# Seven products instead of eight for pairs of groups in the first and last feed-forward half-layers

## The chip, the cores and the metric

One Trainium2 chip, one of its cores. The metric is the time of one execution in microseconds (us) of device time. Times of before: three runs, median 942.07 us.

## The reference, cut to what matters

Two decoder layers over 256 tokens of 1024 features in fp32. Each layer is a half feed-forward, a mixer, and another half feed-forward; that makes four feed-forward halves, numbered f = 0 to 3 in the kernel. The change touches halves 0 and 3.

```python
def _rmsnorm(x, g):
    y = x * lax.rsqrt(jnp.mean(x * x, axis=-1, keepdims=True) + EPS)
    return y * g
def _swiglu(h, w_gate, w_up, w_down):
    return (jax.nn.silu(h @ w_gate) * (h @ w_up)) @ w_down
...
    x = x + 0.5 * _swiglu(_rmsnorm(x, ffn_norm[layer, 0]), ffn_w_gate[layer, 0],
                          ffn_w_up[layer, 0], ffn_w_down[layer, 0])
```

The hidden width is 2816. The first mixer is attention with pooling, the second an S5 state-space layer with a GLU behind it.

## The kernel before

**Tiling.** The 256 tokens are two tiles of 128 (t = 0, 1). The normalized activations stand in `hn[t]` by rows and, transposed, in `hTh` and `hTl`. Every fp32 factor is cut into a high part of reduced precision (fp32r) and the rest, and a product is three products of parts: high by high, high by rest, rest by high. For a weight, ScalarE copies the loaded tile `raw` into `wh` (the high part, line 182) and VectorE subtracts it from `raw` into `wl` (line 139). The factor `rstd` of the norm is applied after the product.

**Groups.** A feed-forward half goes over 11 groups g of 256 hidden columns. For each group and token tile, `gate_up` multiplies the activations by the gate and up columns together (512 columns), in two halves `kh` of the contraction, 4 x 3 matmuls of 128x512 in each half, into a PSUM tile `wk`. Then ScalarE makes `sg` = silu(gate x rstd) (line 436), VectorE makes `pr` = up x rstd x sg (line 148), `hid_T` transposes `pr` on TensorE into `sk` and splits it into `hh` and `hl`, and `down` multiplies these by 256 rows of the down matrix into `acc`, 24 matmuls for the group. `ffn_joint` puts the down products of the group before behind the gate and up products of this one.

**Weights.** A weight unit is 1 MB: gate and up columns of one group and one half of the contraction (`f`), or 256 rows of the down matrix (`d`). It is loaded by two DMAs of 512 KB from SP's queue into `raw` (four buffers) and split by two copies and two subtractions of 128x1024 into `wh` and `wl` (`RING` = four buffers of each). `pump`, called ahead of every step, issues the loads and splits of the next units in the order of first use, as far as the four-deep ring allows: a unit can be split when the unit four before it has had its last use.

**Order.** The program is traced as a list of steps. The order of each engine's queue is then fixed when the program is built: a scheduler goes through its own model of time, and an idle engine gets, among the instructions whose data and buffers are ready, the one with the best priority, which is the one traced first; `prio(n)` moves an instruction n places forward, `behind(...)` pins it behind others on its engine. On the chip each queue runs in that order. VectorE's and ScalarE's work on products (`sg`, `pr`, `hh`, `hl`) carries `prio(CHAIN)` and goes ahead of the splits. PSUM has two `wk` and two `sk` buffers.

**Around the change.** Half 0 begins with `first`, which loads x and the first weights; group 0 follows in separate steps, then `ffn_joint(0, 1, 4)`, a step `opened` that opens the mixer's memory, issues its ten small loads and computes the rotary tables, and `ffn_joint(0, 4, NG)`. Half 3 follows the GLU of the S5 layer: its memory is released, `head(3, "f3")` does group 0, and `ffn_joint(3, 1, NG)` the rest. The weights of the GLU (`in_s_w_glu`) are loaded through the same `raw` buffers.

Of the kernel before, what the change touches and what calls it, by code (L numbers as in the profile page):

```python
# [17 lines left out]
DM = 1024  # L18
# [20 lines left out]
    p600 p101 s10 p610 p701 e00 p601 s11 x10 p710 T00 p611 t10 x11 g0 p711 s00 t12 g1 p400 x00 p401 m0 t01 p410  # L39
    p510 m1 t00 p500 v00 t11 p411 p511 G1 p501 v10 G0 t13 v01 v11 V0 V1 o20 o21 o31 o30  # L40
"""


ORDER = """
# [66 lines left out]
def trunk_kernel(ctx: ExitStack, tc: tile.TileContext, I, out):  # L111
# [119 lines left out]
    def emit_dma(i):  # L231
        kind = units[i // 2][0]
        if kind == "K":
            return
        if kind == "W":
            r = wraw.tile([128, 1024], F32, tag="raw", name="rawW")
            c0 = (i % 2) * 1024
            keep("rawW", SP.dma_start(out=r, in_=s5["dW"][2 + units[i // 2][1]][:, c0:c0 + 1024]))
            raws[i] = r
            return  # L240
        src = pieces(units[i // 2])[1][i % 2][0]
        r = wraw.tile(list(src.shape), F32, tag="raw", name="raw")
        for k in (slice(0, 2), slice(2, 4)) if i == 0 else (slice(None),):
            keep("load", SP.dma_start(out=r[:, k], in_=src[:, k]))
        raws[i] = r

    def raw_busy(i):

        if units[i // 2][0] == "K":
            return False  # L250
        before = [k for k in range(i) if units[k // 2][0] != "K"][-RAW:]
        u = units[before[0] // 2] if before else units[0]
        return u[0] == "W" and last_use[u] >= state["step"]

# [5 lines left out]
    def emit_split(i):  # L260
        if units[i][0] == "K":
            n = units[i][1]
            tl = [wsp.tile([128, 2048], F32, tag=tg, name=f"K{n}") for tg in ("wh", "wl")]
            for q in range(2):
                c0 = 4096 * n + 2048 * q
                with behind("put"):
                    SP.dma_start(out=tl[q], in_=s5["dK"][:, c0:c0 + 2048])
            held[units[i]] = tl
            return
        if units[i][0] == "W":  # L270
            fill(2 * i)
            held[units[i]] = [raws.pop(2 * i + q).rearrange("p (a r j q n) -> p r j q a n", a=2, r=2, j=4, q=2)
                              for q in range(2)]
            return
        shape, places = pieces(units[i])
        h = wsp.tile([128, *shape], F32R, tag="wh", name="wh")
        l = wsp.tile([128, *shape], F32R, tag="wl", name="wl")
        for p in range(2):
            fill(2 * i + p)
            r = raws.pop(2 * i + p)  # L280
            s = places[p][1]
            with behind("split"):
                for k in (slice(0, 2), slice(2, 4)) if i + p == 0 else (slice(None),):
# [6 lines left out]
        held[units[i]] = (h, l)  # L290

    def pump():
        if state["hold"]:
# [119 lines left out]
    def gate_up(f, g, t, kh, ks):  # L413
# [21 lines left out]
        with prio(CHAIN):  # L435
            ACT.activation(out=sg, in_=ps[:, 0], func=AF.Silu, scale=rstds[f, t])  # L436
            stt(pr, ps[:, 1], rstds[f, t], sg, ALU.mult, ALU.mult)
        prods[f, g, t] = pr

    def hid_T(f, g, *ts):  # L440
# [857 lines left out]
    def ffn_joint(f, g0, g1):  # L1298

        for g in range(g0, g1):  # L1300
            paced.add(len(steps))
            for kh in range(2):
                if f == 1 and g == NG - 1 and kh:
                    S(hold)
                for t in range(2):
                    GU(f, g, t, kh)
                    if g == 1 and kh == 0:
                        HID(f, 0, t)
            if g < NG - 1:
                dn(f, g - 1, 0)  # L1310
                HID(f, g, 0, 1)
                dn(f, g - 1, 1)

    def tail(f, fin_a, fin_b, each=lambda t, c: None):
        S(strict(f == 1))
# [52 lines left out]


    def first():  # L1370
        row = hn[1][0:8, 0:128]
        with prio(3 * CHAIN):
            ACT.dma_start(out=ident, in_=cst[:, C_ID:C_ID + 128])
# [67 lines left out]
    tail(0, N(0, "m0"), HT(0))  # L1441
    S(lambda: norm(1, "m0"))

# [115 lines left out]
    S(lambda: h_transpose(0, wk, "glu"))  # L1559
    S(lambda: s5["rp"].release())  # L1560
    S(lambda: s5["pool"].release())
    head(3, "f3")
    ffn_joint(3, 1, NG)
    for t in range(2):
        dn(3, NG - 2, t, (0,))
        if t == 0:
# [4 lines left out]
        for c in range(2):  # L1571
            dn(3, NG - 1, t, (c,))
            S(lambda t=t, c=c: finish(t, c))

    def finish(t, c):
        a = accs[t]
# [9 lines left out]
    early = [("y", 0, 0), ("y", 0, 1), ("W", 0), ("W", 1), ("K", 0), ("K", 1)]  # L1586
    i = min(units.index(u) for u in early)
    units[:] = units[:i] + early + [u for u in units[i:] if u not in early]
    for k, (fn, uids) in enumerate(steps):
        state["step"] = k  # L1590
        if k:
# [33 lines left out]
```

## Time and profile before

| | |
|---|---|
| median of 3 runs (lowest to highest) | 942.07 us (940.71 to 943.63) |
| the profiled execution | 943.62 us, of which its span is 941.9 us |
| TensorE busy / VectorE busy / ScalarE busy | 98% / 69% / 47% of the span |
| weights and other data read from HBM | 173.24 MB, 194 GB/s with what is written |

The span is the time between the first and the last instruction that the profiler saw; the time of the execution lies a little above it. A busy share says how long an engine had something in work, not that it was the one that the others waited for; the chain of waits says that. PE is TensorE's matmuls, PEld its weight loads, DVE is VectorE, ACT ScalarE, POOL GpSimd; SPq is SP's queue, which issues the loads.

### The profile page before, as it was taken

What the parts mean: (1) busy time and instruction counts of PE and PEld (TensorE: products, weight loads), DVE (VectorE), ACT (ScalarE), POOL (GpSimd) and SP (SyncE); (2) the same over time, 40 slices, a digit from 0 to 9 for tenths busy, and PEclk for the clock granted to TensorE, in tenths of its full rate; (3) what the DMA queues carried; (4) which work ended last, traced back from release to release, by engine and by line L of the source; (5) the groups of instructions that cost most, each with busy time, mean ns of one, the idle gap of its engine ahead of it and who ended that gap; (6) DMA issues with size and microseconds to landing.
All of it is one profiled execution on the core that took longest, in us unless ns stands there. A gap on an engine that the chain in (4) does not pass through costs nothing.

```text
span 941.9 us, 13195 instructions
## 1 busy us (share of the span) xinstructions
PE 921.3 (98%) x5001; PEld 763.2 (81%) x5001; DVE 648.5 (69%) x1068; ACT 443.4 (47%) x618; POOL 64.5 (7%) x113
## 2 busy tenths in 40 slices
PE   8999999999999999999999999999879999999998
PEld 6788888889988888888888888888558888888886
DVE  5746654578966659999896548999486675554552
ACT  6544444455546444444464444445335464444440
POOL 0000000013020000000132001600200000000000
PEclk9999999999999999999999999999999999999999
DMA  7867656544476977556788555966945556566641
GB/s 239 269 197 223 193 182 198 194 164 148 134 195 204 198 216 208 179 164 197 241 251 285 180 179 160 266 203 205 300 166 181 177 179 222 180 187 201 192 136 45
DMA packets 149056, 184.59 MB, mean 196 GB/s; under 512 B 23161, under 2 KB 131649, under 8 KB 148225
## 3 DMA queue, kind: packets, MB, share of 16 engines
q1 hardware_dynamic: 145184, 174.70, 60.1%
q0 software_dynamic: 3504, 8.92, 3.8%
q8 instruction: 39, 0.64, 0.3%
q10 hardware_dynamic: 304, 0.14, 0.1%
q14 instruction: 25, 0.20, 0.1%
HBM read 173.24 MB, written 9.44 MB: 194 GB/s over the span
## 4 chain that ended last, share of the span: by engine, by line
PE 82%; DVE 8%; DMA 4%; ACT 2%; issue 2%; POOL 1%; SPq 0%; ACTq 0%; DVEq 0%; POOLq 0%
PE wk L101 50%; PE acc L101 25%; PE sk L101 7%; DVE wl L139 2%; DMA raw<-in_ffn_w_up_dram 2%; DMA V<-x 1%; ACT wh L182 1%; POOL r L621 1%; DVE X L139 1%; DVE b_t L139 1%; DMA raw<-in_ffn_w_gate_dram 1%; DMA raw<-in_s_w_glu_dram 1%; DVE qk L139 0%; ACT h L1090 0%; DVE b_q L139 0%
## 5 line engine op out<-in xcount | busy, mean ns | idle before, releaser
L139 DVE TENSOR_TENSOR wl<-raw,wh 128x1024 fp32r<-128x1024 f32 (+1 forms) x305 | 363.2, 1217 | 165.0 <-ACT wh L182 164.3
L182 ACT ACTIVATE wh<-raw 128x1024 fp32r<-128x1024 f32 (+1 forms) x305 | 309.3, 1051 | 243.4 <-PE wk L101 115.6
L101 PE MATMUL wk<-wh,hTh 128*128 128x512 f32 (+1 forms) x836 | 219.0, 381 | 3.6 <-DVE pr L148 1.5
L101 PE MATMUL wk<-wl,hTh 128*128 128x512 f32 (+1 forms) x836 | 216.1, 377 | 0.0
L101 PE MATMUL wk<-wh,hTl 128*128 128x512 f32 (+1 forms) x836 | 215.1, 377 | 0.0
L101 PEld LDWEIGHTS wk<-wh,hTh 128*128 128x128 f32 x836 | 151.3, 189 | 33.4 <-ACT hTh L182 2.7
L101 PEld LDWEIGHTS wk<-wl,hTh 128*128 128x128 f32 x836 | 152.3, 189 | 28.8 <-DVE wl L139 0.2
L101 PEld LDWEIGHTS wk<-wh,hTl 128*128 128x128 f32 x836 | 152.2, 189 | 28.8
L101 PE MATMUL acc<-wh,hh 128*128 128x512 f32 x352 | 141.4, 402 | 0.0
L101 PE MATMUL acc<-wh,hl 128*128 128x512 f32 x352 | 137.5, 392 | 0.0
L101 PE MATMUL acc<-wl,hh 128*128 128x512 f32 x352 | 137.2, 390 | 0.0
L436 ACT ACTIVATE sg<-wk,rstd 128x256 f32<-128x256 f32 x88 | 41.7, 475 | 111.5 <-PE wk L101 106.9
L148 DVE SCALAR_TENSOR_TENSOR pr<-wk,rstd,sg 128x256 f32<-128x256 f32 x88 | 42.1, 480 | 55.8 <-ACT sg L436 55.8
L101 PEld LDWEIGHTS acc<-wh,hl 128*128 128x128 f32 x352 | 66.0, 188 | 14.9 <-DVE hl L139 0.7
L101 PEld LDWEIGHTS acc<-wl,hh 128*128 128x128 f32 x352 | 66.3, 188 | 12.3
L101 PEld LDWEIGHTS acc<-wh,hh 128*128 128x128 f32 x352 | 66.2, 188 | 12.2 <-issue 0.2
L182 ACT ACTIVATE hh<-sk 128x512 fp32r<-128x512 f32 (+1 forms) x52 | 27.5, 528 | 30.0 <-PE sk L101 30.0
L139 DVE TENSOR_TENSOR hl<-sk,hh 128x512 fp32r<-128x512 f32 (+1 forms) x52 | 31.3, 605 | 4.2 <-ACT hh L182 4.1
L101 PE MATMUL sk<-ident,pr 128*128 128x128 f32 x176 | 28.2, 273 | 0.3 <-DVE pr L148 0.3
L101 PEld LDWEIGHTS sk<-ident,pr 128*128 128x128 f32 x176 | 22.0, 139 | 7.8 <-DVE pr L148 0.8
L978 POOL DMA_DIRECT2D dK<-E x36 | 18.8, 542 | 82.2 <-ACT E L959 72.9
L341 ACT ACTIVATE acc<-x 128x512 f32<-128x512 f32 x24 | 14.3, 597 | 21.4 <-DVE x L148 17.1
(294 smaller groups left out, 627.1 us busy)
## 6 DMA issues: line engine op xcount, KB each, us to landing
raw<-in_ffn_w_up_dram SPq DMA_DIRECT2D x88, 512.0 KB
raw<-in_ffn_w_down_dram SPq DMA_DIRECT2D x88, 512.0 KB
raw<-in_ffn_w_gate_dram SPq DMA_DIRECT2D x87, 512.0 KB
raw<-in_ev_w_in_dram SPq DMA_DIRECT2D x16, 512.0 KB
raw<-in_s_w_glu_dram SPq DMA_DIRECT2D x16, 512.0 KB
raw<-in_ev_w_out_dram SPq DMA_DIRECT2D x8, 512.0 KB
K<-dK SPq DMA_DIRECT2D x4, 1024.0 KB
dK<-E POOLq DMA_DIRECT2D x36, 64.0 KB, 5.0
```

The lines of the kernel that those rows point to most:

```text
L101: i = f(*a, **k)
L139: return DVE.tensor_tensor(out=o, in0=a, in1=b, op=op)
L148: return DVE.scalar_tensor_tensor(out=o, in0=a, scalar=s, in1=b, op0=op0, op1=op1)
L182: return ACT.activation(out=o, in_=i, func=AF.Copy)
L341: keep("square", ACT.activation(out=into or acc_of(t)[c], in_=xs[t][:, s], func=AF.Square, scale=1.0 / 32.0, accum_out=sums[t][:, c:c + 1]))
L436: ACT.activation(out=sg, in_=ps[:, 0], func=AF.Silu, scale=rstds[f, t])
L621: POOL.tensor_tensor(out=r8, in0=s8, in1=mhalf.to_broadcast([128, 8]), op=ALU.pow)
L978: POOL.dma_start(out=dK[16 * tp:16 * tp + 16, :, tau], in_=Kf[16 * (7 - lag):16 * (7 - lag) + 16])
```

## The change

Two neighbouring groups g and g + 1 are taken together as a product of 2x2 blocks: the activations are [a11 a12; a21 a22] (rows: token tiles; columns: halves of the contraction), the weights [b11 b12; b21 b22] (rows: halves of the contraction; columns: groups). Instead of eight block products, seven are formed, some of them of sums of blocks, and the four results are sums of these seven (the scheme of Strassen in Winograd's form). In half 0 this is done for groups 2 and 3, 5 and 6; in half 3 for groups 2 and 3, 5 and 6, 8 and 9. The groups between stay as they were.

- `pair_rows` makes the block sums of the activations by rows, in place in `hn`; the first token tile is scaled by `rho` = rstd of tile 0 over rstd of tile 1, so that the sums may mix the tiles. In half 0 the rows times the gain are made first, with the gain loaded to all partitions. `pair_turn`, four times per half, behind the products of group 1, transposes one block sum and splits it into `sTh` and `sTl`.
- The weights of a pair are four blocks of 1 MB, loaded into four buffers `sr` of their own (`emit_dma`, kind "m"). `split_pair` splits each of the seven factors into `wh` and `wl` like a unit; ahead of the sixth it makes three sums of blocks, each in two operations of 128x1024 on VectorE, ahead of the seventh one more.
- `pair_product` does one product (12 matmuls into `wk`) and adds it to the others: a scaled copy on ScalarE for the first, VectorE operations of 128x512 for the rest, and `gate` where a result is complete.
- The order of the products is 1, then the down products of the group before, then 6, 2, 7, 5, 4, 3; the units are split in the order 1, down, 2, 6, 7, 5, 4, 3.
- The memory `pair` is opened in `first` and released in `opened`, and opened again ahead of `head(3, "f3")`. `opened` moves from ahead of group 4 to ahead of group 7.

```diff
+PAIRS = {0: (2, 5), 3: (2, 5, 8)}
...
     def emit_dma(i):
         kind = units[i // 2][0]
         if kind == "K":
             return
+        if kind == "m":
+            _, f, g, j = units[i // 2]
+            if j > 2:
+                return
+
+            n, kh = j - 1, i % 2
+            r = pr_["pool"].tile([128, 4, 2, 256], F32, tag="sr", name="sr", bufs=4)
+            for q, nm in enumerate(("ffn_w_gate", "ffn_w_up")):
+                SP.dma_start(out=r[:, :, q], in_=I[nm][f // 2, f % 2, kh * 512:(kh + 1) * 512,
+                                                      (g + n) * 256:(g + n + 1) * 256].rearrange("(k p) f -> p k f", p=128))
+            raws[f, g, n, kh] = r
+            return
...
+        if units[i][0] == "m":
+            for p in range(2):
+                fill(2 * i + p)
+            split_pair(units[i])
+            return
...
+    def split_pair(u):
+
+        _, f, g, j = u
+        b11, b21, b12, b22 = (raws.get((f, g, n, kh)) for n in range(2) for kh in range(2))
+        h, l = (wsp.tile([128, 4, 2, 256], F32R, tag=tg, name=tg) for tg in ("wh", "wl"))
+        lf = pr_["t2"]
+        parts = [slice(0, 2), slice(2, 4)]
+        with behind("split"):
+            if j == 6:
+                for k in parts:
+                    tt(b11[:, k], b12[:, k], b11[:, k], ALU.subtract)
+                    tt(lf[:, k], b11[:, k], b22[:, k], ALU.subtract)
+                    tt(b21[:, k], b21[:, k], lf[:, k], ALU.add)
+            if j == 7:
+                for k in parts:
+                    tt(b12[:, k], b22[:, k], b12[:, k], ALU.subtract)
+            r = {1: b11, 2: b21, 3: b22, 4: b21, 5: b11, 6: lf, 7: b12}[j]
+            for k in parts:
+                keep("splits", hi_of(h[:, k], r[:, k]), tt(l[:, k], r[:, k], h[:, k].bitcast(F32), ALU.subtract))
+        held[u] = (h, l)
...
+    def pair_rows(f):
+
+        a11, a12, a21, a22 = (hn[t][:, c * 512:(c + 1) * 512] for t in range(2) for c in range(2))
+        rho = pr_["rho"]
+        if f == 0:
+            gv = pr_["pool"].tile([128, DM], F32, name="pg")
+            SP.dma_start(out=gv, in_=I["ffn_norm"][0, 0].partition_broadcast(128))
+            for t in range(2):
+                for c in range(2):
+                    o = slice(c * 512, (c + 1) * 512)
+                    tt(hn[t][:, o], xs[t][:, o], gv[:, o], ALU.mult)
...
+        tt(a22, a21, a22, ALU.add)
+        stt(a21, a11, rho, a21, ALU.mult, ALU.subtract)
+        stt(a11, a11, rho, a22, ALU.mult, ALU.subtract)
+        stt(a12, a12, rho, a11, ALU.mult, ALU.add)
+
+    def pair_turn(n):
+        t, c = n // 2, n % 2
+        ps = sk((128, 4, 128))
+        h, l = (v[:, 4 * c:4 * c + 4, t * 128:(t + 1) * 128] for v in pr_["T"])
+        with behind("gu"):
+            for k in range(4):
+                tr(ps[:, k], hn[t][:, (4 * c + k) * 128:(4 * c + k + 1) * 128], ident)
+            hi_of(h, ps)
+            tt(l, ps, h.bitcast(F32), ALU.subtract)
+
+    def pair_product(f, g, j):
+        w = held["m", f, g, j]
+        S, X = pr_["T"], (hTh, hTl)
+        src, c, t = {1: (X, 0, 0), 2: (X, 1, 0), 3: (S, 1, 0), 4: (X, 1, 1), 5: (S, 1, 1), 6: (S, 0, 0), 7: (S, 0, 1)}[j]
+        ps = wk((128, 2, 256))
+        o = slice(t * 128, (t + 1) * 128)
+        for x, y in ((src[0], w[0]), (src[0], w[1]), (src[1], w[0])):
+            for k in range(4):
+                keep("gu", mm(ps, x[:, 4 * c + k, o], y[:, k], k == 0 and x is src[0] and y is w[0], k == 3 and x is src[1]))
+        s1, u2, u3, u5 = pr_["u"]
+        with prio(CHAIN):
+            if j == 1:
+                ACT.activation(out=s1, in_=ps, func=AF.Copy, scale=pr_["rho"])
+            elif j == 6:
+                tt(u2, ps, s1, ALU.add)
+            elif j == 2:
+                stt(s1, ps, pr_["rho"], s1, ALU.mult, ALU.add)
+                gate(f, g, 0, s1)
+            elif j == 7:
+                tt(u3, ps, u2, ALU.add)
+            elif j == 5:
+                tt(u5, ps, u3, ALU.add)
+                gate(f, g + 1, 1, u5)
+                tt(u2, ps, u2, ALU.add)
+            elif j == 4:
+                tt(u3, ps, u3, ALU.add)
+                gate(f, g, 1, u3)
+            else:
+                tt(u2, ps, u2, ALU.add)
+                gate(f, g + 1, 0, u2)
...
+                    if g == 1 and f in PAIRS:
+                        S(lambda n=2 * kh + t: pair_turn(n))
...
+            for j in (1, 0, 6, 2, 7, 5, 4, 3):
+                if j:
+                    S(lambda j=j, g=g: pair_product(f, g, j), ("m", f, g, j))
+                else:
+                    for t in range(2):
+                        dn(f, g - 1, t)
+            HID(f, g, 0, 1)
+            dn(f, g, 0)
+            HID(f, g + 1, 0, 1)
+            dn(f, g, 1)
+            g += 2
...
     def first():
+        pair_open(0)
...
-    ffn_joint(0, 1, 4)
+    S(lambda: pair_rows(0))
+    ffn_pairs(0, 1, 7)
 
     def opened():
+        pr_["pool"].release()
...
-    ffn_joint(0, 4, NG)
+    ffn_joint(0, 7, NG)
...
+    S(lambda: pair_open(3))
     head(3, "f3")
-    ffn_joint(3, 1, NG)
+    S(lambda: pair_rows(3))
+    ffn_pairs(3, 1, NG)
```

## Rows read from the trace of the kernel before

**Rows 1.** The page's busy times: engine, busy us, share of the span, instructions.
```profile
PE 921.3 (98%) x5001; PEld 763.2 (81%) x5001; DVE 648.5 (69%) x1068; ACT 443.4 (47%) x618; POOL 64.5 (7%) x113
```

**Rows 2.** The chain of waits, half 3: start us, us, engine, tile, count.
```profile
798.23 10.88 PE wk L101 x48
815.02 10.88 PE wk L101 x48
```

**Rows 3.** Busy time by stretch: us, each engine's, PE clock, DMA share, GB/s.
```profile
58.70:75.49 16.79, 16.79 (x77) 13.90 (x76) 8.63 (x9) 7.47 (x9) 0.00 (x0) 1.00 0.59 184
80.00:100.00 20.00, 20.00 (x92) 16.55 (x91) 15.12 (x65) 9.47 (x11) 0.00 (x0) 1.00 0.79 251
360.00:460.00 100.00, 99.66 (x451) 82.15 (x450) 98.59 (x228) 44.73 (x53) 0.55 (x1) 1.00 0.61 182
768.00:781.00 13.00, 13.00 (x61) 10.70 (x61) 10.12 (x12) 7.96 (x10) 0.00 (x0) 1.00 0.93 297
```

**Rows 4.** The timeline of PE, one hidden transpose: start us, us, instruction, count.
```profile
778.10 0.60 PE L101 MATMUL sk<-ident,pr 128*128 128x128 f32 x4
...
778.77 0.39 PE L101 MATMUL acc<-wl,hh 128*128 128x512 f32 x1
```

**Rows 5.** The groups of instructions by shape: count, busy us, mean ns, idle before.
```profile
L139 DVE TENSOR_TENSOR wl<-raw,wh 128x1024 fp32r<-128x1024 f32 x303 | 361.8, 1221 | 164.4 <-ACT wh L182 163.7
L182 ACT ACTIVATE wh<-raw 128x1024 fp32r<-128x1024 f32 x303 | 308.0, 1054 | 240.7 <-PE wk L101 115.6 <-PE acc L101 73.8 <-DMA raw<-in_ffn_w_up_dram 16.0
...
L148 DVE SCALAR_TENSOR_TENSOR pr<-wk,rstd,sg 128x256 f32<-128x256 f32 x88 | 42.1, 480 | 55.8 <-ACT sg L436 55.8
...
L139 DVE TENSOR_TENSOR hl<-sk,hh 128x512 fp32r<-128x512 f32 x36 | 24.8, 689 | 1.0 <-ACT hh L182 0.9
...
L182 ACT ACTIVATE hh<-sk 128x512 fp32r<-128x512 f32 x36 | 21.5, 597 | 24.3 <-PE sk L101 24.3
```

**Rows 6.** The timeline of DVE, two stretches without a gap.
```profile
711.75 4.63 DVE L139 TENSOR_TENSOR wl<-raw,wh 128x1024 fp32r<-128x1024 f32 x4
...
750.15 1.29 DVE L139 TENSOR_TENSOR hTl<-wk,hTh 128x512 fp32r<-128x512 f32 x2 [1.87 <-ACT hTh L182]
```

**Rows 7.** The timelines of POOL and of SP's queue.
```profile
0.88 0.20 POOL L1503 MEMSET warm<- 128x128 bf16 x1
...
267.96 0.34 SPq L783 DMA_DIRECT2D b_im<-in_cst_dram  x1
...
303.04 0.42 SPq L759 DMA_DIRECT2D b_araw<-in_s_a_re_dram  x1
```

**Rows 8.** The timeline of the start: SP's loads, and group 1's first matmuls.
```profile
4.91 1.20 SPq L244 DMA_DIRECT2D raw<-in_ffn_w_up_dram  x1
...
9.03 0.37 SPq L244 DMA_DIRECT2D raw<-in_ffn_w_gate_dram  x1
...
11.57 0.37 SPq L244 DMA_DIRECT2D raw<-in_ffn_w_up_dram  x1
...
24.45 1.20 PE L101 MATMUL wk<-wh,hTh 128*128 128x512 f32 x4 [1.53 <-DVE pr L148]
```

**Rows 9.** Busy time by stretch, as rows 3: the start, the S5 layer.
```profile
4.00:8.00 4.00, 2.08 (x7) 1.39 (x7) 2.15 (x4) 1.61 (x3) 0.00 (x0) 1.00 0.98 315
8.00:12.00 4.00, 3.67 (x17) 3.67 (x18) 1.92 (x2) 1.33 (x2) 0.00 (x0) 1.00 1.08 370
...
20.00:24.00 4.00, 2.92 (x13) 2.07 (x12) 1.93 (x5) 3.99 (x10) 1.35 (x7) 1.00 0.86 244
...
700.00:704.00 4.00, 3.42 (x78) 2.36 (x81) 3.39 (x5) 2.59 (x4) 0.00 (x0) 0.74 0.01 4
```

**Rows 10.** The timeline ahead of half 3: last reads, GLU loads, first use.
```profile
707.76 1.03 PE L101 MATMUL sk<-ident,V 128*128 128x128 f32 x8
...
713.00 12.68 SPq L244 DMA_DIRECT2D raw<-in_s_w_glu_dram  x8
...
729.51 1.07 PE L101 MATMUL wk<-wh,hTh 128*128 128x512 f32 x4
```

More of the change, by code (lines that the diff above doesn't have):

```diff
@@ L247, in raw_busy @@
     def raw_busy(i):
-        if units[i // 2][0] == "K":
+        if units[i // 2][0] in "Km":
             return False
-        before = [k for k in range(i) if units[k // 2][0] != "K"][-RAW:]
+        before = [k for k in range(i) if units[k // 2][0] not in "Km"][-RAW:]
         u = units[before[0] // 2] if before else units[0]
@@ L290, in emit_split @@
         held[units[i]] = (h, l)
+    pr_ = {}
+    def split_pair(u):
[17 more added lines that the diff above has]
+        held[u] = (h, l)
     def pump():
@@ L437, in gate_up, with pair_open @@
             stt(pr, ps[:, 1], rstds[f, t], sg, ALU.mult, ALU.mult)
+        prods[f, g, t] = pr
+    def pair_open(f):
+        pr_["pool"] = p = tc.alloc_tile_pool(name="pair", bufs=1)
+        pr_["T"] = [p.tile([128, 8, SEQ], F32R, name=nm) for nm in ("sTh", "sTl")]
+        pr_["u"] = [p.tile([128, 2, 256], F32, name=f"u{n}") for n in range(4)]
+        pr_["t2"] = p.tile([128, 4, 2, 256], F32, name="t2")
+        pr_["rho"] = p.tile([128, 1], F32, name="prho")
+    def pair_rows(f):
[8 more added lines that the diff above has]
+                    tt(hn[t][:, o], xs[t][:, o], gv[:, o], ALU.mult)
+        root = pr_["pool"].tile([128, 1], F32, name="root")
+        POOL.tensor_tensor(out=root, in0=rstds[f, 1], in1=mhalf, op=ALU.pow)
+        tt(rho, rstds[f, 0], root, ALU.mult)
+        tt(rho, rho, root, ALU.mult)
+        tt(a22, a21, a22, ALU.add)
+        stt(a21, a11, rho, a21, ALU.mult, ALU.subtract)
+        stt(a11, a11, rho, a22, ALU.mult, ALU.subtract)
+        stt(a12, a12, rho, a11, ALU.mult, ALU.add)
@@ L438, in gate_up, with gate @@
+    def gate(f, g, t, z):
+        sg = tmp.tile([128, 256], F32, tag="t256", name="sg")
+        pr = pr_["pool"].tile([128, 256], F32, tag="pp", name="pp", bufs=4)
+        ACT.activation(out=sg, in_=z[:, 0], func=AF.Silu, scale=rstds[f, 1])
+        stt(pr, z[:, 1], rstds[f, 1], sg, ALU.mult, ALU.mult)
         prods[f, g, t] = pr
@@ L1312, in ffn_joint, with ffn_pairs @@
                 dn(f, g - 1, 1)
+    def ffn_pairs(f, g0, g1):
+        g = g0
+        while g < g1:
+            if g not in PAIRS[f]:
+                ffn_joint(f, g, g + 1)
+                g += 1
+                continue
+            for j in (1, 0, 6, 2, 7, 5, 4, 3):
[9 more added lines that the diff above has]
+            g += 2
     def tail(f, fin_a, fin_b, each=lambda t, c: None):
@@ L1573, in trunk_kernel @@
             S(lambda t=t, c=c: finish(t, c))
+    S(lambda: pr_["pool"].release())
     def finish(t, c):
@@ L1588, in trunk_kernel @@
     units[:] = units[:i] + early + [u for u in units[i:] if u not in early]
+    for f in PAIRS:
+        for g in PAIRS[f]:
+            a, b = (units.index(("m", f, g, j)) for j in (6, 2))
+            units[a], units[b] = units[b], units[a]
     for k, (fn, uids) in enumerate(steps):
```

## The prediction

> **What bounds the kernel now.** I read the busy times first: TensorE is busy 98% of the span, VectorE 69%, ScalarE 47% [rows 1]. The reader should not stop there, because a busy share is an average. The chain of waits says it more sharply: through the last feed-forward half it is one piece of 48 matmuls after another, 10.88 us each, 16.8 us from start to start, with no other engine between [rows 2]. One group of the hidden width is therefore 16.79 us of TensorE, and in that stretch TensorE is busy all of the time while VectorE works 8.63 us and ScalarE 7.47 us [rows 3]. So TensorE's columns set the time in the two layers that the change touches, and VectorE has about 8 us in 17 to give.
>
> **What is removed.** A pair of groups has eight products of blocks now (two token tiles, two halves of the contraction, two groups), 12 matmuls each. Seven remain. One matmul takes 10.88 / 48 = 0.2267 us [rows 2], a product 2.72 us. Five pairs (two in the first half-layer, three in the last) save 5 x 2.72 = 13.6 us.
>
> **What is added on TensorE.** Eight turns of four 128x128 transposes, four for each half-layer, bring the block sums of the activations into place. In the trace four transposes and the matmul behind them go from 778.10 to 778.77, 0.67 us, less 0.23 for the matmul: 0.44 us a turn [rows 4]. Eight turns cost 3.5 us. TensorE thus gains 13.6 - 3.5 = 10.1 us, and this is the most that the change can give.
>
> **What is added on VectorE.** Per pair: three more weight units (six subtractions of 128x1024), eight block sums of 128x1024, and seven sums of products of 128x512. The nearest rows: a 128x1024 tensor-tensor lasts 1.22 us, a 128x512 one 0.69 us, the gate product 0.48 us, a hidden split 0.69 us [rows 5]. Back to back they overlap: four in 4.63 us and two of 512 in 1.29 us [rows 6], so some 1.14 and 0.60 us each in a full queue; the gate product, with the same overlap of 0.08, counts 0.40 us. I count the block sums, which mostly read what the one before wrote, at 1.22 us. A pair and the single group behind it is the period in which VectorE must keep up:
> 24 halves x 1.14 + 8 sums x 1.22 + 7 x 0.60 + 6 gates x 0.40 + 3 hidden splits x 0.60 = 45.5 us, against TensorE's 3 x 16.79 - 2.72 = 47.6 us. At full durations the same list is 48.8 us, more than TensorE has. VectorE goes from half idle to the edge, and the order within a pair decides.
>
> I walk one pair, T = 0 at its first product, by due times on TensorE: product 1 from 0, the down products of the group before from 2.72, then products 6, 2, 7, 5, 4, 3 from 8.16, 10.88, 13.60, 16.32, 19.04 and 21.76, transposes at 24.48, down from 24.9. A unit can be split once the unit four before it has been used. Unit 2 therefore waits for the last gate and up half before the pair, used up at T = -5.9 (one down of 5.44 us and 0.44 us of transposes ahead of 0). From there VectorE has one gate product (0.40), ScalarE's lead on the first half (0.8 more), unit 2 (2.28), six block sums (7.3) and a hidden split (0.6): 5.5. Unit 6 is ready at 7.8, due 8.16. Unit 7 with two sums and a sum of products: 13.1, due 13.60. Unit 5 behind one sum and a gate: 16.4, due 16.32. Unit 4: 19.3, due 19.04. Unit 3 behind 1.6 us of product 5's sums: 23.2, due 21.76, but its low half only 0.9 us later: about 0.5 us late. Then the hidden transposes come: ScalarE's copy 0.60 us and VectorE's rest 0.69 us [rows 5] lie between them and the first down matmul, 1.5 us with the waits, and behind them TensorE has only what is split of the next group; I count half of it, 0.8 us. So 1.3 us are lost per pair, 6.5 us for five.
>
> Bounds: below, nothing. For 100 us of the second half-layer VectorE is busy 98.59 us and TensorE still 99.66 us [rows 3], so a full VectorE queue need not hold TensorE up; but there most of the filling could wait, and here it is due in order. Above, at full durations the walk ends with unit 3 at 24.9 instead of 23.2, 2.3 us late, with 1.5 us behind it: 3.8 us per pair, 19 us. I take 1.3, by the overlap seen in rows 6.
>
> The Trainium skill ("VectorE: DVE Perf Modes", The DRAIN you can't avoid) says that the next vector operation does not start until the pipe of the one before has emptied. By that rule the full durations would stand and the sum below would come to +12 us instead of -0.6; four operations within 4.63 us, where four full durations are 4.88, speak against it here [rows 6]. That rule is behind the second rival below.
>
> ScalarE gets six copies of 1.05 us and one of about 0.6 us more per pair [rows 5], 7 us in 31, on top of twice 7.47: it stays under the other two. The rows of activation sums (four operations for each half-layer, four more for the gain in the first) and the turns' halves are 8 to 12 operations of 0.60 us; they fall into group 1, where VectorE has about 8 us free. In the last half-layer it is busy 10.12 of the 13 us ahead of 781 [rows 3], so if that cover fails up to 5 us come on top; I take none.
>
> **What is moved.** The step that loads the mixer's tables goes from before group 4 to before group 7, with its ten loads on SP and its small VectorE operations: the 20 us that hold them now show 65 operations and 15.12 us, about 5 us more than a plain group's share [rows 3]. Four single groups (67 us) still lie between it and the mixer that reads the tables, and these have VectorE half idle: nothing. Its POOL memsets wait for nobody.
>
> **The loads.** The bytes are the same; their place isn't. The four blocks of a pair land in four buffers of their own, eight loads of 512 KB. Nothing holds the first four back but the memory, and the trace shows what the schedule does with such work: a memset of the S5 stage, line 1503, runs at 0.88 us, and a load of line 783 goes out at 267.96 us, 35 us ahead of the loads of line 759, which stand before it in the program [rows 7]. So I expect these loads, and the broadcast gain of 0.5 MB, in SP's queue right behind the first four weight loads, where SP is free from 6.1 to 9.03 us [rows 8]. Ahead of group 1's loads (issued at 9.03 and 11.57 us) then stand up to 4.7 MB. The queue moved 315 to 370 GB/s there [rows 9]: x and group 0, 3.15 MB, are in by about 12 us (2.74 MB of it moved from 4 to 12), the 4.7 MB by 24.8 to 27, group 1's first two by 27.6 to 30.3, and with 1.2 us for the split TensorE starts group 1 at 28.8 to 31.5 instead of 24.45 [rows 8]. That is 4.3 to 7 us, and nothing if they are issued behind. If some go ahead and others not, about 3 us, which I take. Later the same queue has less to do, but TensorE no longer waits for it there.
>
> In the last half-layer the memory comes free at about 709 us, ahead of the eight GLU loads issued from 713.00 [rows 10]. The 4.2 MB take 11 to 13 us, the next two GLU loads land near 725 us, are split by 728, and their matmuls start at 729.51: covered, with 1 to 2 us to spare. Without that cover 3 us; I take none.
>
> **Sum.** -13.6 + 3.5 + 6.5 + 3.0 = -0.6 us. The profiled run took 943.62 us (a span of 941.9 us and 1.7 us around it), so 943.0 for a run like it; it lay 1.55 us over the median of 942.07, and against that median the sum is 941.5 us. Runs of before spread by 0.3%, 2.8 us, which is about what can be told from no change.
>
> **Rivals.**
> First, faster: VectorE keeps up as it does at 360 to 460 us and the early loads cost nothing or little. For it: the walk is only 0.5 us late at unit 3, and VectorE has been seen full beside a full TensorE. Against it: the due order. It gives 942.1 - 10.1 and up to 6 us of small losses: 932 to 939 us. Chance 0.35.
> Second, slower by VectorE: each operation costs its full duration of rows 5, or waits in the queue behind a sum whose product is late. For it: VectorE's list at full durations is over TensorE's period. Against it: the overlap in rows 6. It decides from 2 us a pair on. 942.1 - 10.1 + 19 + 3 = 954 us; at half of the excess 948. Chance 0.16.
> Third, slower by the start: all 4.7 MB go ahead of group 1 at the lower rate: 942.1 - 10.1 + 6.5 + 7 = 945.5 us. TensorE then idles some 7 us; where it was broken up by waits, at 700 to 704 us, the granted clock was 0.74 [rows 9], between its levels of 1.2 and 2.4 GHz, and a few us at such a clock would add 1 to 2: 947 us. The Trainium skill ("TensorE: Matmul & The Clock Gate", HAM oscillation) warns of just such gaps; at the start of this trace the waits of 20 to 24 us left the clock at 1.00 [rows 9]. Chance 0.13.
>
> **How the numbers follow.** No change within 0.3%, 939.3 to 944.9 us: 0.36, with 941.5 the sum. Faster 0.35, slower 0.16 + 0.13 = 0.29. The range for 8 in 10 leaves out about 1 in 10 at each end: 934 to 952 us. The likeliest case alone spans 939 to 945.
>
> **What would show it.** In the profile after: 60 fewer matmuls of 128x512 and 32 more transposes; VectorE at 90% or more in the pairs' stretches; TensorE idle 1 to 2 us behind each product 3, ahead of the down products, released by a hidden split or a weight subtraction. At the start, the eight loads between SP's first loads and group 1's, and TensorE idle at 25 to 28 us on a load of in_ffn_w_gate or w_up. The prediction is wrong if the pairs lose more than 3 us each, or if group 1 starts at 24.5 us and the pairs lose nothing.

## The result, and the profile after

The change makes the kernel slower: median 950.91 us (949.2 to 952.35, four runs) against 942.26 us (940.71 to 943.63, four runs). The ratio is 1.0091, with a 95% interval of 1.007 to 1.0111, so about 8.6 us more where no change was forecast. The two profiled executions lie closer, 949.2 and 943.62 us: that of after was its fastest run, that of before its slowest. The stages below are compared between these two, 5.6 us apart. The measured 950.91 us lies inside the predicted 934 to 952 us, but at the slow end, which stood for other mechanisms than the one found here; that it does is luck.

The page of after, busy times and slices (answers to [rows 1]):

```profile
PE 916.3 (97%) x4973; PEld 756.9 (80%) x4973; DVE 758.1 (80%) x1197; ACT 481.2 (51%) x661; POOL 65.5 (7%) x115
...
PE   7789999999999999999999999999779999999998
...
PEclk9889999999999999999999999999999999999999
```

A slice is 23.7 us. TensorE works less than in before, as it should, and the kernel is longer. The reader should look at slices two and three: they are not full, and the granted clock is down. That is 24 to 71 us, the beginning of the first half-layer. The change's other place, the last half-layer, shows nothing of the kind.

Waits of TensorE in after, from 20 to 60 us:

```profile
PE sk L103 <- DVE h L150: 7.3, 1, 7.3
PE wk L103 <- DVE pr L150: 2.3, 1, 2.3
```

One wait of 7.3 us stands out, for an operation on `h` at line 150, the helper of scalar-tensor-tensor: a sum of activations in `pair_rows`. Its place on TensorE's timeline:

```profile
41.59 1.07 PE L103 MATMUL wk<-wh,hTl 128*128 128x512 f32 x4
50.01 0.47 PE L103 MATMUL sk<-ident,h 128*128 128x128 f32 x1 [7.35 <-DVE h L150]
...
54.96 0.63 PE L103 MATMUL acc<-wh,hh 128*128 128x512 f32 x1
...
57.52 0.62 PE L103 MATMUL wk<-wh,sTh 128*128 128x512 f32 x2
```

Product 1 of the first pair ends at 42.66 us. Next in TensorE's queue is the first turn, and behind it everything else. VectorE's timeline over the same stretch says why it had to wait:

```profile
36.00 2.36 DVE L141 TENSOR_TENSOR wl<-raw,wh 128x1024 fp32r<-128x1024 f32 x2 [0.47 <-ACT wh L184]
38.72 2.36 DVE L141 TENSOR_TENSOR wl<-sr,wh 128x1024 fp32r<-128x1024 f32 x2 [0.36 <-ACT wh L184]
40.99 1.22 DVE L141 TENSOR_TENSOR sr<-sr 128x1024 f32<-128x1024 f32 x1
42.13 2.49 DVE L141 TENSOR_TENSOR h<-x,pg 128x512 f32<-128x512 f32 x4
44.54 1.22 DVE L141 TENSOR_TENSOR t<-sr 128x1024 f32<-128x1024 f32 x1
45.67 0.68 DVE L141 TENSOR_TENSOR h<-h 128x512 f32<-128x512 f32 x1
46.27 1.22 DVE L141 TENSOR_TENSOR sr<-sr,t 128x1024 f32<-128x1024 f32 x1
47.41 0.75 DVE L150 SCALAR_TENSOR_TENSOR h<-h,prho,h 128x512 f32<-128x512 f32 x1
48.07 1.22 DVE L141 TENSOR_TENSOR sr<-sr 128x1024 f32<-128x1024 f32 x1
49.21 0.74 DVE L150 SCALAR_TENSOR_TENSOR h<-h,prho,h 128x512 f32<-128x512 f32 x1
```

The rows times the gain come at 42.13 us, behind four splits and a sum of weights; then the sums of activations alternate with sums of weights that are not due until later. The one that the first turn needs is done at 49.95 us. No operation here waits for a load. But the gain `pg` was issued late, at 29.32 us, behind six loads of the first pair's blocks on SP:

```profile
27.23 0.84 SPq L245 DMA_DIRECT2D sr<-in_ffn_w_gate_dram  x1
28.12 1.15 SPq L245 DMA_DIRECT2D sr<-in_ffn_w_up_dram  x1
29.32 0.65 SPq L499 DMA_DIRECT2D pg<-in_ffn_norm_dram  x1
```

Busy time by stretch (columns as in [rows 3]; the number ahead of the DMA's two is the granted clock):

```profile
24.00:28.00 4.00, 3.79 (x10) 3.02 (x11) 3.95 (x5) 2.33 (x3) 0.00 (x0) 0.61 0.85 287
40.00:44.00 4.00, 2.66 (x12) 1.88 (x10) 4.00 (x6) 0.69 (x1) 0.00 (x0) 1.00 1.05 378
44.00:48.00 4.00, 0.00 (x0) 0.00 (x0) 4.00 (x6) 1.06 (x1) 0.00 (x0) 0.67 0.29 93
48.00:52.00 4.00, 1.99 (x8) 1.66 (x9) 4.00 (x7) 1.05 (x2) 0.00 (x0) 0.50 0.00 0
52.00:56.00 4.00, 4.00 (x15) 3.17 (x14) 3.66 (x5) 1.36 (x3) 0.00 (x0) 0.55 0.00 0
...
783.00:831.00 48.00, 47.78 (x220) 39.12 (x220) 46.82 (x52) 29.37 (x36) 0.00 (x0) 1.00 0.58 189
831.00:879.00 48.00, 47.78 (x217) 39.07 (x216) 46.80 (x50) 29.02 (x35) 0.00 (x0) 1.00 0.65 209
```

VectorE is full from 40 to 52 us while TensorE stands idle from 42.66 to 50.01 us: a busy engine working on the wrong thing first. Behind the idle time the granted clock is 0.50 to 0.55, the lower of the two levels (1.2 of 2.4 GHz), until 56 us. From 50.01 to 57.52 us TensorE does 12 matmuls, four turns and two transposes, 2.7 + 1.8 + 0.2 = 4.7 us by the prices of the prediction, in 7.5 us: 2.8 us for the clock. The same on a small scale at 24 to 28 us, where group 1 begins behind a wait of 2.27 us and its first 12 matmuls take 4.44 us (24.21 to 28.65 us) instead of 2.86, at a granted clock of 0.61. That wait is for a gate product `pr`, and in VectorE's queue another wait stands ahead of it, 1.29 us for POOL's part of `rho`:

```profile
22.26 0.16 DVE L141 TENSOR_TENSOR prho<-rstd,root 128x1 f32<-128x1 f32 x1 [1.29 <-POOL root L505]
...
23.68 0.48 DVE L150 SCALAR_TENSOR_TENSOR pr<-wk,rstd,sg 128x256 f32<-128x256 f32 x1
```

In gain_first, below, `rho` comes at 27.72 us, behind that gate product, and the wait is 0.29 us; no run moves `rho` alone. The last two lines of the table of stretches are stretches of the last half-layer, each as long as a pair and a single group: VectorE is busy 97.5% of them, and TensorE idle for 0.22 us in each.

Three stages show where the time went. The first half-layer ends with VectorE's first update of x from `acc` (192.7 us in before); the last one is measured from the first four matmuls of its group 1 (763.95 us in before) to the last update (938.0 us). The ratio rests on all runs of a kernel and is not quite the quotient of the medians given below; the stages come from one profiled run each, which can lie off the median (938.5 us for gain_first, 947.28 us for pairs_later). One run of later_gain_first, in a slower state of the chip, is left out of its ratio.

| kernel | ratio to before (95%) | first half-layer ends | then to last group 1 | from there to the end |
|---|---|---|---|---|
| before | 1 | 192.7 | 571.2 | 174.1 |
| after | 1.0091 (1.007 to 1.0111) | 202.3 | 571.8 | 169.5 |
| last_only | 0.9979 (0.9963 to 0.9996) | 192.0 | 571.9 | 170.7 |
| first_only | 1.0129 (1.0109 to 1.0149) | 201.5 | 574.2 | 174.1 |
| gain_first | 0.9982 (0.9965 to 0.9998) | 192.4 | 571.5 | 169.1 |
| pairs_later | 1.0005 (0.999 to 1.0021) | 195.9 | 576.3 | 169.5 |
| rows_ahead | 1.0069 (1.0044 to 1.0093) | 199.0 | 574.4 | 171.2 |
| stall_warm | 1.0043 (1.0027 to 1.0058) | 199.3 | 572.0 | 169.9 |
| no_sums | 0.9951 (0.992 to 0.9982) | 188.9 | 574.5 | 170.8 |
| pool_sums | 1.0189 (1.0155 to 1.0223) | 200.2 | 576.2 | 181.6 |
| later_gain_first | 0.995 (0.9925 to 0.9975) | 190.0 | 571.4 | 170.3 |
| hid_early | 0.9978 (0.9957 to 0.9998) | 192.7 | 574.0 | 170.9 |
| later_hid | 0.9974 (0.9955 to 0.9993) | 192.6 | 575.3 | 170.2 |
| turns_only | 1.0023 (1.0006 to 1.0039) | 192.2 | 572.1 | 176.8 |

In after the first half-layer costs 9.6 us, the last gives 4.6 back, 0.6 come between: 5.6. The stretch between holds nothing of the change but the first block loads of the last half-layer, and yet varies by 5 us among these kernels, and first_only, without these loads, has 3 us more there than before; TensorE's wait for the rearranged x at the start of the S5 stage (`wk` for `h`, line 139 in before) is 2.7 us in before, 4.3 in after and 1.4 to 6.8 in the others. So the outer columns are the sharper measure.

### The profile page after: what moved, and what is told of

It is laid out like the page before. It is cut to its first block, busy times and chain, and to the rows that moved or that the text cites. A ratio compares the mean times of both kernels' runs of the same rounds, so it can differ in the third digit from the quotient of the medians.

```text
span 947.4 us, 13313 instructions
## 1 busy us (share of the span) xinstructions
PE 916.3 (97%) x4973; PEld 756.9 (80%) x4973; DVE 758.1 (80%) x1197; ACT 481.2 (51%) x661; POOL 65.5 (7%) x115
## 4 chain that ended last, share of the span: by engine, by line
PE 75%; DVE 15%; DMA 4%; issue 3%; ACT 2%; POOL 1%; SPq 0%; DVEq 0%; ACTq 0%; POOLq 0%
PE wk L103 43%; PE acc L103 24%; PE sk L103 7%; DVE wl L141 5%; DMA raw<-in_ffn_w_up_dram 2%; DVE sr L141 1%; DVE h L141 1%; ACT wh L184 1%; POOL r L742 1%; DMA V<-x 1%; DVE X L141 1%; DVE b_t L141 1%; DMA raw<-in_ffn_w_down_dram 1%; DMA raw<-in_ffn_w_gate_dram 1%; DVE pr L150 0%
## 5 line engine op out<-in xcount | busy, mean ns | idle before, releaser
L141 DVE TENSOR_TENSOR wl<-raw,wh 128x1024 fp32r<-128x1024 f32 (+1 forms) x265 | 316.3, 1216 | 81.3 <-ACT wh L184 80.1
L184 ACT ACTIVATE wh<-raw 128x1024 fp32r<-128x1024 f32 (+1 forms) x265 | 270.2, 1052 | 185.1 <-PE wk L103 72.7
L103 PE MATMUL wk<-wh,hTh 128*128 128x512 f32 (+1 forms) x736 | 193.0, 380 | 3.8 <-DVE pr L150 2.3
L103 PE MATMUL wk<-wl,hTh 128*128 128x512 f32 (+1 forms) x736 | 190.6, 377 | 0.0
L103 PE MATMUL wk<-wh,hTl 128*128 128x512 f32 (+1 forms) x736 | 189.3, 376 | 0.0
L103 PEld LDWEIGHTS wk<-wh,hTh 128*128 128x128 f32 x736 | 132.4, 190 | 29.0 <-DVE pr L150 2.7
L103 PEld LDWEIGHTS wk<-wh,hTl 128*128 128x128 f32 x736 | 133.9, 190 | 25.0
L103 PEld LDWEIGHTS wk<-wl,hTh 128*128 128x128 f32 x736 | 133.8, 190 | 25.0
L141 DVE TENSOR_TENSOR wl<-sr,wh 128x1024 fp32r<-128x1024 f32 x60 | 71.4, 1219 | 5.5 <-ACT wh L184 5.4
L184 ACT ACTIVATE wh<-sr 128x1024 fp32r<-128x1024 f32 x60 | 60.5, 1052 | 20.3 <-DVE sr L141 7.9
(323 smaller groups left out, 937.4 us busy)
```

What stands on the lines that cost most here:

```text
L103: i = f(*a, **k)
L141: return DVE.tensor_tensor(out=o, in0=a, in1=b, op=op)
L184: return ACT.activation(out=o, in_=i, func=AF.Copy)
```

## The experiments

**Which half-layer loses?** Pairs in one of the two alone.

```diff
-PAIRS = {0: (2, 5), 3: (2, 5, 8)}
+PAIRS = {3: (2, 5, 8)}
```

The kernel last_only has this line, first_only has `PAIRS = {0: (2, 5)}`; the steps that only the other half-layer needs go with it.

> Pairs only in the last half-layer (three), none in the first; the tables' step stays where the change put it. Theory of the stall: the loss of the change sits in the first half-layer, where TensorE's turns wait for the sums of activations; the last half-layer by itself gained 4.6 us between the traces of before and after (it ends 5.6 us late after starting 10.2 us late). So 4.6 us faster than the kernel before, 937 to 938.5 us. Rival of VectorE: every pair costs about 3.7 us of waits (18.7 us over five pairs, the 8.6 us measured plus the 10.1 us saved), so three pairs and the turns give 3 x (3.7 - 2.72) + 1.76 = 4.7 us slower, 947 us.

> Pairs only in the first half-layer (two), none in the last. Theory of the stall: about 9.6 us slower than the kernel before, as far as the end of that half-layer came late in the trace of after, and up to 13 if the medians hold: 952 to 955 us, slower than the whole change. Rival of VectorE: 2 x (3.7 - 2.72) + 1.76 = 3.7 us slower, 946 us.

Measured: 940.3 and 955.24 us against 942.86 of before. The last half-layer by itself gains 2.0 us in the ratio and 3.4 us in its own stage, less than the 4.6 expected (TensorE waits 1.7 us once for ScalarE's copy `hh`); the first one alone loses 12.2, as expected. The rival, by which all pairs lose alike, is out: it had the sign of the first of these wrong, and the size of the second by 8.5 us.

**Is it the stall?** Three kernels take it apart. In gain_first only the load of the gain is made earlier:

```diff
...
-            gv = pr_["pool"].tile([128, DM], F32, name="pg")
-            SP.dma_start(out=gv, in_=I["ffn_norm"][0, 0].partition_broadcast(128))
+            gv = pr_["pg"]
...
     def first():
...
         x_transpose(0, 0)
+        pr_["pg"] = pr_["pool"].tile([128, DM], F32, name="pg")
+        with behind("load"):
+            SP.dma_start(out=pr_["pg"], in_=I["ffn_norm"][0, 0].partition_broadcast(128))
```

> The whole change, with the broadcast gain of 0.5 MB loaded right behind x instead of behind six loads of the first pair's blocks; the sums of activations then come ahead of the first sums of weights in VectorE's queue. Theory of the stall: TensorE's 7.35 us of idle time ahead of the first turn and the 2.8 us at a low clock behind it go, and the 0.5 MB hold group 0 and group 1 up by 1.5 us: 8.6 - 10.1 + 1.5 = 0 against the kernel before, 940 to 944 us. Rival of VectorE: the idle time only moves into the pairs, and the time stays near 951 us.

Measured: 941.17 us, ratio 0.9982. Only the load has moved, to 4.48 us on SP:

```profile
3.14 1.29 SPq L1534 DMA_DIRECT2D x<-in_x_dram  x2
4.48 0.44 SPq L1538 DMA_DIRECT2D pg<-in_ffn_norm_dram  x1
```

With that the scheduler puts the rows times the gain between 12.45 and 20.47 us and the sum that the first turn needs at 34.81 us, ahead of all sums of weights; the first turn, now at 35.61 us, waits 0.72 us. TensorE and its clock in the stretch of the stall:

```profile
40.00:44.00 4.00, 4.00 (x23) 3.36 (x22) 4.00 (x6) 2.63 (x4) 0.00 (x0) 1.00 1.06 382
44.00:48.00 4.00, 4.00 (x19) 3.31 (x18) 4.00 (x5) 0.69 (x1) 0.00 (x0) 1.00 0.39 130
48.00:52.00 4.00, 4.00 (x20) 3.30 (x19) 4.00 (x5) 2.12 (x2) 0.00 (x0) 1.00 0.02 6
```

The first half-layer ends 9.9 us earlier than in after, by the expected mechanism, and the whole kernel is a little faster than before. That 9.9 is so near the 10.2 of the stall and its clock is partly chance: the same edit cut TensorE's wait ahead of group 1 from 2.27 to 0.29 us and kept the clock at 1.00 there, while TensorE's waits for `wl`, 1.5 us in four, are new.

In stall_warm 30 matmuls of zeros stand behind product 1 of the first pair:

```diff
+        if (f, g, j) == (0, 2, 1):
+            with behind("gu"):
+                warm(30, pr_["w"])
...
```

> The whole change, with 30 matmuls of zeros (128x512, bf16) put on TensorE between the first product and the first turn, where TensorE stood idle for 7.35 us; their results go nowhere. They fill about 6.6 us and can't shorten the wait itself. If the slow matmuls behind the wait (7.5 us from 50.0 to 57.5 us for 4.7 us of work) come from the clock that the idle time cost, the granted clock stays at 1.00 and the kernel is 2 to 3 us faster than the change, 948 to 949 us. If they are slow for another reason (waits hidden in them), nothing changes: 951 us.

```profile
44.00:48.00 4.00, 4.00 (x21) 1.75 (x19) 4.00 (x6) 1.06 (x1) 0.00 (x0) 1.00 0.19 61
48.00:52.00 4.00, 3.85 (x20) 2.30 (x19) 4.00 (x6) 1.59 (x3) 0.00 (x0) 1.00 0.00 0
```

The same wait, filled with work that nobody needs: the clock stays at 1.00, the first half-layer ends 3.0 us earlier than in after, and the median is 947.42 us (1.0043 against 1.0091). The 2.8 us worked out above are the clock's. This agrees with the Trainium skill ("TensorE: Matmul & The Clock Gate", HAM oscillation), which describes a kernel whose waits for DMAs between stretches of matmuls make the next stretch start at the lower clock; here the wait was for VectorE.

In rows_ahead the first sums of weights are pinned behind the last sum of activations:

```diff
-        with behind("split"):
+        with behind("split", *(["rows"] if f == 0 and j == 6 else [])):
...
-        stt(a12, a12, rho, a11, ALU.mult, ALU.add)
+        keep("rows", stt(a12, a12, rho, a11, ALU.mult, ALU.add))
```

> The whole change, its gain loaded where the change loads it; only the order in VectorE's queue differs: the first pair's sums of weights stand behind the sums of activations instead of among them. If the landing of the gain (issued at 29.3 us) sets the stall, the rows still start late and TensorE still idles 5 us or more ahead of the first turn: at most 2 us less than the change, 949 us. If VectorE's order sets it (in the trace of after, two splits of raw, two of sr and one sum, 5.9 us, stand ahead of the rows and three sums of 1.14 us among them), the rows end 3.4 us or more earlier, the idle time falls from 7.35 us to 4 us or less and less clock is lost: 4 to 6 us less than the change, 945 to 947 us.

Measured: 950.46 us, 1.0069. The expected 945 to 947 us was missed, and the median hardly differs from the change's; the stage does. The rows come at 39.72 us, again straight behind the splits and with no wait for the load, and the first turn waits 3.18 us instead of 7.35. The first half-layer ends 3.3 us earlier than in after, but 1.3 us of that stand ahead of the stall: group 1 kept its clock of 1.00 here (product 1 ends at 41.39 us, not 42.66). Part of what was won at the stall goes again: TensorE then waits 0.9, 0.4 and 0.4 us for `pr`, `pp` and `u` later in the half-layer, where after has 0.7 and 0.2, and the clock is 0.50 at 44 to 48 us. So the order in VectorE's queue does set the wait, and the wait is shorter by 4.2 us, but pinning one step by hand was worth 3.3 us in the stage where the earlier load was worth 9.9.

**Is the place too early?** Pairs and turns one group later, without and with the early gain.

```diff
-PAIRS = {0: (2, 5), 3: (2, 5, 8)}
+PAIRS = {0: (3, 6), 3: (2, 5, 8)}
...
-                    if g == 1 and f in PAIRS:
+                    if f in PAIRS and g == PAIRS[f][0] - 1:
...
```

> The first half-layer's pairs are groups 3 and 4, 6 and 7 instead of 2 and 3, 5 and 6, and its turns stand in group 2 instead of group 1; the tables' step goes behind group 7. Theory of the stall: the sums of activations have a group more of time, so the idle 7.35 us, the 2.8 us at a low clock and part of the 1.2 us of group 1 go: 8.6 - 10.2 and up to 1.2 less, 1.6 to 2.8 us faster than the kernel before, 939.5 to 941 us. Rival of VectorE: as the change, near 951 us.

Measured: 943.43 us, 1.0005: 2 to 3 us worse than the theory of the stall had it. The turns' stall is gone, but group 1 begins behind a wait of 2.8 us for `pr`, the granted clock is 0.76 at 24 to 28 us and 0.81 at 28 to 32, TensorE waits another 2.1 us for copies `hh`, and the first half-layer ends at 195.9 us. I had counted part of the loss at group 1 as gone. With the early gain it is:

> The gain loaded first, and the first half-layer's pairs one group later (3 and 4, 6 and 7; turns in group 2). With the gain first and the pairs in the place of the change the first half-layer ended 0.3 us earlier than before where 3.7 us were to be had, and without the sums of weights 3.8 us earlier. If the 3.4 us are lost because VectorE comes into the first pair with the splits of the start still in its queue, a single group more ahead of it gives 1 to 3 us back: 938 to 940 us, 0.3 to 0.5% faster than before. If a pair's work in VectorE's queue is too much wherever it stands, nothing comes back: 941 us.

Measured: 939.85 us, 0.995 (0.9925 to 0.9975): faster than before by 0.5%, with the lowest ratio of the kernels that do all of the work; its interval overlaps that of gain_first. The wait ahead of group 1 is 0.3 us, and from there through the turns and most of the first pair TensorE has no idle time:

```profile
24.00:36.00 12.00, 12.00 (x55) 9.56 (x54) 11.25 (x17) 7.42 (x11) 0.00 (x0) 1.00 0.89 278
36.00:48.00 12.00, 12.00 (x61) 9.94 (x60) 8.71 (x9) 7.28 (x9) 0.00 (x0) 1.00 0.99 350
48.00:60.00 12.00, 12.00 (x60) 9.91 (x59) 11.57 (x14) 6.18 (x10) 0.00 (x0) 1.00 0.75 258
60.00:72.00 12.00, 12.00 (x54) 9.95 (x53) 11.96 (x12) 7.80 (x9) 0.00 (x0) 1.00 0.04 7
```

The first half-layer ends 2.7 us earlier than in before, of 3.7 that two pairs and four turns can give.

**What do the pairs themselves lose?** Three edits on the kernel with the early gain. First, no_sums leaves the sums of weights out:

```diff
-            if j == 6:
+            if j == 6 and not NOSUM:
...
-            if j == 7:
+            if j == 7 and not NOSUM:
...
```

> The kernel with the gain loaded first, without the eight sums of weights of each pair (the units are split from the blocks as they are, so the products take other weights): VectorE has 9.8 us less to do in each pair. Against that kernel (941.2 us, 0.18% faster than before): if VectorE's load is what the pairs still lose (1.4 us of 6.4 us in the last half-layer, 3.4 us of 3.7 us in the first), up to 4.8 us go, 936.5 to 938.5 us. If the rest is lost to something else (the turns, the latency from the hidden transposes to the down products), less than 1 us goes, 940 to 941 us.

Measured: 938.75 us, 0.9951. Both answers are right, each in one place. In the first half-layer 3.5 us go (192.4 to 188.9 us), all that was missing there: VectorE's load, 1.7 us a pair. In the last one nothing goes (169.1 to 170.8 us), though VectorE has 9.8 us less to do per pair.

In pool_sums two of a pair's eight sums go to POOL:

```diff
-                    tt(b12[:, k], b22[:, k], b12[:, k], ALU.subtract)
+                    POOL.tensor_tensor(out=b12[:, k], in0=b22[:, k], in1=b12[:, k], op=ALU.subtract)
...
```

> The kernel with the gain loaded first, with two of a pair's eight sums of weights (those of the seventh unit, 128x1024 each) on POOL, which is idle 93% of the time in the trace of after. If VectorE's load is what the pairs lose, 2.4 us a pair come off it and the kernel is 0.5 to 2 us faster than that one, 939 to 940.7 us. If POOL takes much longer than VectorE's 1.22 us, or slows VectorE down while it runs, unit 7 comes late, and the kernel is 1 to 5 us slower, 942 to 946 us. No row of the traces so far shows POOL at such a size.

Measured: 962.35 us, 1.0189, far past the worse of the two answers. POOL's rows by group, and the timeline of three of them with the operations beside and behind them:

```profile
L328 POOL TENSOR_TENSOR sr<-sr 128x1024 f32<-128x1024 f32 x10 | 36.8, 3693 | 169.5 <-DVE sr L141 85.6 <-DMA raw<-in_ffn_w_down_dram 46.9 <-ACT wh L184 36.9
```
```profile
46.09 8.94 POOL L328 TENSOR_TENSOR sr<-sr 128x1024 f32<-128x1024 f32 x1 [22.94 <-DVE sr L141]
49.34 2.35 DVE L141 TENSOR_TENSOR sr<-sr,t 128x1024 f32<-128x1024 f32 x2
51.61 1.22 DVE L141 TENSOR_TENSOR wl<-t,wh 128x1024 fp32r<-128x1024 f32 x1
55.06 1.06 ACT L184 ACTIVATE wh<-sr 128x1024 fp32r<-128x1024 f32 x1 [5.62 <-POOL sr L328]
57.12 1.22 PE L103 MATMUL wk<-wh,sTh 128*128 128x512 f32 x2 [4.00 <-ACT wh L184]
...
790.26 2.42 POOL L328 TENSOR_TENSOR sr<-sr 128x1024 f32<-128x1024 f32 x1 [21.59 <-DVE sr L141]
790.50 3.27 DVE L141 TENSOR_TENSOR t<-sr 128x1024 f32<-128x1024 f32 x1
...
799.58 3.31 POOL L328 TENSOR_TENSOR sr<-sr 128x1024 f32<-128x1024 f32 x1 [6.90 <-DVE sr L141]
800.56 3.42 DVE L141 TENSOR_TENSOR t<-sr 128x1024 f32<-128x1024 f32 x1
```

POOL's operation takes 3.69 us on the mean, three times VectorE's 1.22, but the one at 790.26 us only 2.42, twice. VectorE's sum, begun beside that one, ends at 793.77 us, 1.1 us behind POOL's end at 792.68; the one begun at 800.56 us ends at 803.98, again 1.1 us behind POOL's end at 802.89. That is what it would take if it stood still until POOL was done. It goes the other way round too: VectorE works without a gap from 44.80 to 52.83 us, and POOL's operation begun at 46.09 ends at 55.03, 2.2 us behind that stretch. ScalarE waits 5.62 us for it, and TensorE 4.00 us for ScalarE. The Trainium skill ("SBUF — State Buffer", Who interferes with whom) says that a vector operation with two inputs in SBUF contends with a POOL operation that reads SBUF, and that the one that comes second is blocked, not slowed; these rows agree. In the last half-layer TensorE waits 4.9 us for `pr`, and how much of the 19 us in all is POOL's own length and how much the standing still was not separated.

In hid_early a pair's first hidden transposes stand ahead of product 3, in later_hid too, with the pairs one group later:

```diff
             for j in (1, 0, 6, 2, 7, 5, 4, 3):
                 if j:
+                    if j == 3:
+                        HID(f, g, 0, 1)
...
-            HID(f, g, 0, 1)
             dn(f, g, 0)
```

> The gain loaded first, and the hidden transposes of a pair's first group put ahead of product 3 instead of behind it (its gates are done with product 4). If the copy of the hidden sums behind product 3 costs what the prediction took (0.8 us a pair, two of five pairs show TensorE waiting on ScalarE's copy in the trace of after), up to 2 us go: 939 to 940.5 us. If the schedule already fills that time with other groups' matmuls, nothing changes: 941 us.

> Both of these edits on the kernel with the gain first. If both mechanisms hold, their savings add: 937 to 939.5 us. If neither does, 941 us.

Measured: 942.4 us (0.9978) and 941.21 us (0.9974). Neither gains on the kernel without the edit (0.9982 and 0.995); in the second TensorE waits 2.2 us for a copy `hh` in the first half-layer, where later_gain_first has 0.7 us. So the time behind product 3 was not lost for want of this order.

**What do the turns cost?**

```diff
-PAIRS = {0: (2, 5), 3: (2, 5, 8)}
+PAIRS = {3: ()}
...
```

> No pair anywhere; the last half-layer keeps the sums of activations and the four turns, whose results nothing reads. By the prediction's term the turns cost 4 x 0.44 = 1.76 us and the sums nothing: 944 to 944.5 us where before gives 942.5, group 1 to the end of the last half-layer 1.8 us longer. If the sums of activations are not hidden in that half-layer, up to 5 us more: 946 to 949 us.

Measured: 945.64 us, 1.0023 (1.0006 to 1.0039), 2.2 us; the last stage is 2.7 us longer, with one wait of 0.7 us in it for a hidden rest `hl`; 2.0 us are left for the 1.76 predicted. The term of the turns holds, and in this half-layer the sums of activations are hidden, but for that wait at most.

## Why the prediction was wrong

- **What bounds the kernel, what is removed, what the turns cost:** right. The trace has 60 fewer 128x512 matmuls (three times 732 on `wk` became three times 632 and three times 80) and 32 more transposes of `h`, and turns_only gives 2.0 us for 1.76, 2.7 with a wait.
- **The step that failed:** "The rows of activation sums ... fall into group 1, where VectorE has about 8 us free ... I take none." VectorE did have idle time (2.25 and 0.47 us at 33 to 36 us alone). But the order of its queue is fixed when the program is built; with the gain loaded behind six blocks, the rows were placed behind four splits and among the sums of weights, and TensorE's queue stands still at a turn. The cost was 7.35 us of waiting and 2.8 us of clock, 10.2 us, where the text had 0, and 5 us as its bound in the other half-layer only. The error was to ask how much free time VectorE has, and not where in its queue the sums stand and what on TensorE waits for them in order. gain_first shows this step: with nothing but the load moved, the stall and its slow clock are gone and the first half-layer ends 9.9 us earlier. stall_warm gives the clock's share by itself.
- **The loads:** the wrong mechanism, and the size was off in the same sum. I took 3.0 us for block loads ahead of group 1's. They were issued from 15.82 us on, between the others, and group 1 began at 24.21 us, not late. By its clock it came out 1.2 us late even so: its gate and up products end at 37.06 us instead of 36.01, with one piece of hidden transposes (0.14 us) left for later. TensorE had reached it 1.0 us earlier than in before, and the longer wait has behind it VectorE's wait for POOL on account of `rho`, a term that the prediction did not have. The gain's load, which I had counted among these bytes, did its harm by its place in the order.
- **VectorE in the pairs:** 1.3 us a pair predicted. In after the last half-layer gains 4.6 us of 6.4, so 0.6 a pair. In the first, 9.6 = -3.7 + 1.2 + 7.35 + 2.8 + the rest, which leaves 1.9, about 1 a pair. 3.7 us for 6.5: the order of size was right, and the term too large by 2.8 us. In the first half-layer the idle time of the stall probably also gave VectorE time to catch up, which no run shows by itself; in gain_first, without the stall, 3.4 us are lost there, 1.7 a pair, and no_sums gives them back. The place was not right: of the 1.8 us lost in the last half-layer 0.4 show as idle time, at the copies of the hidden sums, and no_sums shows that VectorE's sums are not the cause there. What the other 1.4 us are stays open; they lie in TensorE's busy time, at a granted clock of 1.00.
- **The moved step and the last half-layer's loads:** 0, as predicted; last_only has the moved step and ends its first half-layer at 192.0 us.
- **The sum** of the two profiled executions is -10.1 + 3.7 + 7.35 + 2.8 + 1.2 + 0.6 = 5.6 us; it closes because 1.9 us of the 3.7 are what was left over. Without the failed step it would have been -4.6 us.
- **The rivals:** the third had the right end and nearly the right idle time (some 7 us and a low clock, 947 us), but put it at group 1 and on the weights' loads. The second, VectorE too slow, is out in the last half-layer: 97.5% busy and 0.22 us of idle TensorE in 48. In the first, with the stall gone, VectorE's load does cost 1.7 us a pair, under the 2 us from which that rival was to decide. The first rival is what the kernel comes near once the stall is gone: a ratio of 0.9982 in gain_first, and 0.995, 937.4 us against the median of 942.07, with the pairs one group later. Neither sign of being wrong came true to the letter, but group 1 did start in time and the pairs did lose little, which pointed away from both mechanisms that I had priced.

## What to carry to other kernels

Free time on an engine hides new work only if the work stands in the queue before that time is over: find what the new operation waits for, down to its load, and the first instruction on the bounding engine that waits for it. An idle stretch of TensorE can cost more than its length, since the matmuls behind it may run at the lower clock: here 7.35 us of waiting cost 2.8 us more. When an edit saves work in two places and the total is worse, measure the places by themselves, by stage: here one had gained all along.

## What was not expected of the hardware

A subtraction of 128x1024 took 2.35 to 8.94 us on POOL against 1.22 on VectorE. A VectorE sum begun beside it ended 1.1 us behind it (3.42 us instead of 1.22), and one on POOL begun within a full stretch of VectorE ended 2.2 us behind that stretch (8.94 us). A wait of 2.27 us ahead of group 1 left the granted clock at 0.61 over the next 4 us in after, where 1.53 us in before [rows 8] and 2.0 us in rows_ahead left it at 1.00. And a stage that no edit touched, the start of the S5 layer, took up to 5 us more or less from one profiled kernel to the next, with TensorE's wait for the rearranged x between 1.4 and 6.8 us; why was not tried.
